# A decoder trunk's SSD layer: old states read four at a time, the first gate's tiles between the third group's, and the convolution's history by DMA

## The chip, the cores and the metric

The kernel runs on one core of one Trainium2 chip and is launched once. The metric is the device time of that core in microseconds (us); lower is better. Three runs of the kernel before took 1497.01, 1497.63 and 1501.10 us (median 1497.63). The profiled execution took 1500.51 us.

## The reference

The program is one inference step of a decoder trunk with four layers: a mixer with mLSTM and GLA heads, an MLP, a Mamba-2 (SSD) mixer, and an MLP, each followed by a layernorm of the scaled residual. It works on a prompt of 512 tokens and, at the same time, on 8 sequences ("samples") that each bring 4 new tokens and their old states. All 544 tokens pass through the same weights. The change is in the SSD mixer and in the last layernorm. The mixer computes, with 32 heads of 64 in 4 groups of 8 heads, a state of 128, and a causal convolution over 4 tokens:

```python
z, xbc, dtr = _split(x @ w_in, (SSD_INNER, SSD_CONV_DIM, SSD_HEADS))     # 2048, 3072, 32
cat = jnp.concatenate([conv0, xbc], axis=1)                              # 3 old inputs ahead
conv = conv_b
for w in range(SSD_CONV):
    conv = conv + cat[:, w:w + T] * conv_w[w]
new_conv = cat[:, T:]                                                    # an output
xs, Bm, Cm = _split(jax.nn.silu(conv), (2048, 512, 512))
dt = softplus(dtr + dt_bias);  a = dt * -exp(a_log)
# per chunk, with cs = cumsum(a), h0 the state before it
w = exp(cs[t] - cs[s]) (s <= t) * dt[s]
y = (Cm @ Bm^T * w) @ x  +  (Cm @ h0) * exp(cs)
h = exp(cs[-1]) * h0 + sum(exp(cs[-1] - cs) * dt * x * Bm)               # an output
y = (y + d_skip * xs) * silu(z), normed by group, @ w_out
```

For a sample the chunk is its 4 tokens, and h0 is its own old state: per group of heads a matrix of 128 x 512 floats (256 KB), 8 of them for the 8 samples.

## The kernel before

Activations lie with features on the partitions and tokens along the free side: a tile is 128 features x 544 tokens (512 of the prompt and 32 of the samples), done in two halves of 272 tokens. A dense product of one 128 x 128 weight block with one half is three matmuls of split operands (`dense`, line 367: high x high, low x high, high x low parts). One weight tile of the SSD's input product is 8 such blocks and two halves: 48 matmuls. The weight tiles come by DMA on SP's queue into three raw buffers (`WeightStream`, line 165); ACT makes the high part (line 166) and DVE the low part (line 167).

The stages follow each other: the first mixer (to about 240 us), an MLP (to about 650), the SSD's input product and its chunks (653 to about 1000), its output product, a second MLP, and the last layernorm (from 1486).

In the SSD stage the order of the instructions on TensorE (PE) is the order in which the program writes them (`manual_schedule` for PE). On the other engines, and on the DMA queues, a planner that simulates a timeline sets the order. The program writes dense matmuls, and `tick()` ahead of each of them counts down in "lanes": generators of small work (`dt`, `ssd`, `smp`, `norm`) that yield the number of dense matmuls until they go on (the table `W`: 72 at the start of a group, 14 between chunk steps, 26 between sample steps, 48 ahead of the samples' outputs). A lane works on one generator at a time; the next one in the same lane waits behind it. `until(key)` goes through lanes at once until a result is there.

The weight tiles of the input product come in the order: dt, then for each group g four tiles of x, one of B, one of C. Behind the third group's come the four z tiles of `gate(0)`, then the fourth group's six, then the z tiles of gates 1, 2 and 3. `gate(g)` makes z, its SiLU and the product with Y of group g.

- `ev_conv` (lines 1502 to 1533) is the way out of PSUM for x, B and C: ACT copies the two halves into a tile `ci` that holds three zeros, the prompt, and per sample three old inputs and four new ones (lines 1511, 1514, 1516); POOL fills in the old inputs from `cv0` (1510), and stores the new history to `ncp` and `cv0` (1520, 1521); ACT makes the first tap (1524), DVE three more (1526), and both make the SiLU (1529 to 1532). There are two `ci` buffers. `cv0` is read by one DMA ahead of the stage; two DMAs at the end of the stage write both histories out.
- `group` (1538 to 1661) does one group's four chunks of 128 tokens, and as a fifth block (b = 4) the 32 tokens of the samples. `scores(b)` loads the decay sums broadcast from a DRAM scratch tensor (`E`, line 1563, and for b = 1 to 3 two DMAs for `ec`, line 1568, all on ACT's queue), transposes x (`xt`, 1571), multiplies C and B (`cb`, 1573), and makes the masked matrix E. `state(b)` carries the state (1607, 1610), `outputs(b)` makes y (`yp`, 1632; added to Y at 1635).
- `samples` (1663 to 1697) works through the 8 samples of a group, two per step. A step loads two old states `h0` (line 1670; four buffers) and the same in the other layout, `h0n` (1672), waits 26 dense matmuls, multiplies C with the two old states into rows 64 to 127 of one PSUM tile `it` (1679; 32 rows each, the products of all steps added up: the matrix `Cm` is zero outside the tokens of its sample), makes the state update (`sps`, 1686), adds it on DVE (1692) and writes the new states from POOL's queue (1693). Rows 64 to 127 of `it`, times exp(cs) (`ecs`), go into the lower half of the tile z of block 4 (1694); the lower half of its E holds two unit matrices (`seye`), so that the 16 instructions of `outputs(4)` add the old states' share in the same products.
- `last_layernorm` (474 to 554) makes sums with PE, then works on ACT, DVE and POOL in an order written by hand (`do`, line 525), and issues the output DMAs (552 to 554).

## Time and profile before

| | us |
|---|---|
| median of 3 runs | 1497.63 |
| profiled execution | 1500.51 |
| its span (first to last instruction) | 1498.8 |
| PE busy in the span | 1473.0 |
| DVE busy | 1097.6 |
| ACT busy | 793.8 |
| POOL busy | 226.6 |

All times below are microseconds from the start of the span. An engine's busy time counts its instructions, not its register work or its DMA issues; a "q" behind an engine's name (ACTq, SPq) is its sequencer, where DMA issues and waits are seen. PEld is the load of a weight block into PE, which overlaps the matmuls. "<-DVE h0n L1692" behind an idle time says that it ended when DVE's instruction of line 1692 on the tile h0n was done. The granted clock is the share of full speed that TensorE's clock had in a stretch. fp32 matmuls appear as two instructions each.

### The profile page before, as it was taken

Reading aid. Unit: us, or ns where it says so; the run is one execution under the profiler, and the core shown is the slowest. Engines: PE = TensorE matmul, PEld = TensorE weight load, DVE = VectorE, ACT = ScalarE, POOL = GpSimd, SP = SyncE. Lnnn points to the kernel's source line nnn. Section 1 sums busy time; section 2 is a strip of 40 time slices with the busy share of each in tenths; the row PEclk is TensorE's granted clock in tenths of the full one; section 3 lists DMA queues with packets and bytes.
Section 4 is the critical chain, followed back from the end, with each engine's and each line's share of the span. In section 5 each row is a group of like instructions: output and inputs, shape, how many; then the busy total and the mean of one; then the engine's idle time right before and its main releaser. Section 6 shows DMA issues by size and latency. Waiting matters only on the chain.

```text
span 1498.8 us, 29214 instructions
## 1 busy us (share of the span) xinstructions
PE 1473.0 (98%) x11637; PEld 1423.6 (95%) x11637; DVE 1097.6 (73%) x2072; ACT 793.8 (53%) x1747; POOL 226.6 (15%) x295
## 2 busy tenths in 40 slices
PE   9999999999999999999999999999999999999997
PEld 9999999999999999999888788899999999999996
DVE  4956576886776766578898988777688677676656
ACT  5645556573554453457875675555257354444333
POOL 0511231100000000014444353421010000000000
PEclk9999999999999999999999999999999999999998
DMA  6321325223332232434566766364222233233121
GB/s 226 94 71 58 117 71 168 69 71 97 98 99 86 98 99 58 154 131 130 134 182 195 239 178 217 99 213 143 72 75 71 95 100 99 86 99 99 58 85 60
DMA packets 88225, 172.11 MB, mean 115 GB/s; under 512 B 9224, under 2 KB 43656, under 8 KB 87832
## 3 DMA queue, kind: packets, MB, share of 16 engines
q1 hardware_dynamic: 54968, 139.81, 30.1%
q10 hardware_dynamic: 29760, 17.46, 4.5%
q0 software_dynamic: 3360, 12.98, 2.2%
q8 instruction: 91, 1.49, 0.4%
q14 instruction: 46, 0.38, 0.1%
HBM read 153.48 MB, written 16.73 MB: 114 GB/s over the span
## 4 chain that ended last, share of the span: by engine, by line
PE 89%; DVE 5%; DMA 3%; ACT 2%; issue 1%; POOL 0%; ACTq 0%; DVEq 0%; POOLq 0%
PE psd L367 61%; PE psd L562 18%; DMA E<-d_cs 2%; PE num L812 1%; PE yp L1632 1%; PE gs L1043 1%; DVE acc L1526 1%; PE sp L1610 1%; DVE wlo L167 1%; PE it L1679 1%; PE ip L1607 1%; ACT whi L166 1%; PE sps L1686 1%; PE supd L950 0%; DMA d_ecs<-rows 0%
## 5 line engine op out<-in xcount | busy, mean ns | idle before, releaser
L367 PE MATMUL psd<-xh,whi 128*128 128x272 f32 x1504 | 446.2, 297 | 2.4 <-ACT ci L1516 2.1
L367 PE MATMUL psd<-xh,wlo 128*128 128x272 f32 x1504 | 440.1, 293 | 0.6 <-DVE wlo L167 0.6
L367 PE MATMUL psd<-xl,whi 128*128 128x272 f32 x1504 | 438.3, 291 | 1.5 <-DVE xl L451 1.3
L367 PE MATMUL psd<-hh,whi 128*128 128x272 f32 x1024 | 295.9, 289 | 0.7 <-ACT hh L286 0.7
L367 PE MATMUL psd<-hlo,whi 128*128 128x272 f32 x1024 | 295.5, 289 | 0.2
L367 PE MATMUL psd<-hh,wlo 128*128 128x272 f32 x1024 | 295.4, 288 | 0.0
L367 PEld LDWEIGHTS psd<-xh,whi 128*128 128x128 f32 x1504 | 283.8, 189 | 9.8 <-issue 5.1
L367 PEld LDWEIGHTS psd<-xl,whi 128*128 128x128 f32 x1504 | 284.3, 189 | 7.5 <-issue 4.2
L367 PEld LDWEIGHTS psd<-xh,wlo 128*128 128x128 f32 x1504 | 283.7, 189 | 4.8 <-issue 2.8
L167 DVE TENSOR_TENSOR wlo<-wraw,whi 128x1024 fp32r<-128x1024 f32 (+2 forms) x173 | 207.4, 1200 | 60.0 <-ACT whi L166 59.1
L166 ACT CAST whi<-wraw 128x1024 fp32r<-128x1024 f32 (+2 forms) x173 | 174.2, 1011 | 131.8 <-PE psd L367 114.4
L367 PEld LDWEIGHTS psd<-hh,whi 128*128 128x128 f32 x1024 | 192.8, 188 | 1.3 <-ACT hh L286 1.2
L367 PEld LDWEIGHTS psd<-hlo,whi 128*128 128x128 f32 x1024 | 192.8, 188 | 0.8 <-DVE hlo L287 0.6
L367 PEld LDWEIGHTS psd<-hh,wlo 128*128 128x128 f32 x1024 | 192.7, 188 | 0.1
L401 DVE TENSOR_TENSOR xf<-xf,psd 128x272 f32<-128x272 f32 x208 | 88.1, 432 | 76.0 <-PE psd L367 75.4
L562 PE MATMUL psd<-xh,wlo 128*128 128x272 f32 x416 | 119.9, 288 | 0.0
L562 PE MATMUL psd<-xh,whi 128*128 128x272 f32 x416 | 119.8, 288 | 0.0
L562 PE MATMUL psd<-xl,whi 128*128 128x272 f32 x416 | 119.6, 288 | 0.0
L202 ACT CAST whi<-wsum 128x1024 fp32r<-128x1024 f32 x52 | 54.3, 1044 | 111.3 <-PE psd L562 70.1
L202 ACT CAST whi<-wraw 128x1024 fp32r<-128x1024 f32 (+1 forms) x52 | 43.4, 834 | 95.3 <-PE psd L367 84.2
L203 DVE TENSOR_TENSOR wlo<-wsum,whi 128x1024 fp32r<-128x1024 f32 x52 | 63.7, 1224 | 23.2 <-ACT whi L202 23.2
L562 PEld LDWEIGHTS psd<-xl,whi 128*128 128x128 f32 x416 | 78.4, 188 | 0.0
(477 smaller groups left out, 2820.8 us busy)
## 6 DMA issues: line engine op xcount, KB each, us to landing
wraw<-mlp_w SPq DMA_DIRECT2D x80, 512.0 KB, 3.7
wraw<-ssd_in SPq DMA_DIRECT2D x40, 512.0 KB, 4.0
wraw<-mlp_w SPq DMA_DIRECT2D x64, 256.0 KB, 3.0
wraw<-ab_in SPq DMA_DIRECT2D x24, 512.0 KB, 3.7
h<-h SPq DMA_DIRECT2D x32, 256.0 KB, 3.9
h0n<-h0n SPq DMA_DIRECT2D x16, 512.0 KB, 4.5
E<-d_cs ACTq DMA_DIRECT2D x16, 512.0 KB, 4.3
s_h<-h0n POOLq DMA_DIRECT2D x16, 512.0 KB, 4.3
```

The source lines that it names most:

```text
L166: nc.scalar.copy(hi[:, r], w[:, r])
L167: nc.vector.tensor_tensor(lo[:, r], w[:, r], hi[:, r].bitcast(F32), ALU.subtract)
L202: self.cut[0] = nc.scalar.copy(hi, x).ins
L203: self.cut[1] = nc.vector.tensor_tensor(lo, x, hi.bitcast(F32), ALU.subtract).ins
L367: last[0] = TE.matmul(ps[:, :TH], wt[:, k, :], rt, start=i == 0, stop=i == n - 1).ins
L401: V.tensor_tensor(x, x, ps, ALU.add)
L562: last[0] = TE.matmul(ps, wt[:, k], bt[:, k], start=first and n == 0, stop=n == 11, skip_group_check=not first).ins
L812: TE.matmul(num[i], sT[:, i] if j == i else sT[:, (4, 7, 9)[j] + i - j - 1], vt[key][:, j, h, :w], start=j == 0, stop=j == i)
L1043: TE.matmul(p[:, 2 * m * b:2 * m * (b + 1)].rearrange("p (e t) -> p e t", e=2), z[:, 2 * m * b:2 * m * b + P], zq[:, :, m * b:m * (b + 1)] ...
L1526: V.scalar_tensor_tensor(acc[:, :n], ci[:, w:w + n], cw[:, m, w:w + 1], acc[:, :n], ALU.mult, ALU.add)
L1607: TE.matmul(ip[:, j * P:(j + 1) * P], hT[:, j * P:(j + 1) * P], Cf[:, tk], start=True, stop=True)
L1610: TE.matmul(sp, Bt[:, b], xw, start=True, stop=True)
```

## The change

Five parts are changed together.

1. Old states are read four at a time: in every second sample step four matmuls go to four blocks of 32 rows of `it` (0 to 127), and none in the others. `it` times `ecs` (now for four blocks of rows) goes into a tile `zs` of its own, taken from the `h0` buffers, and `outputs(4)` has eight more matmuls, `zs` with `seye`, accumulated with the former ones. E and z of block 4 become tiles that are zeroed once; the copies of `seye` and the zero fills per group go.
2. `gate(0)` becomes a generator. The weight order of the third group was x, x, x, x, B, C, launch of the group's chunks, z, z, z, z; it is now x, x, x, x, z, B, z, C, z, z, launch. The host lays out the weights in that order.
3. The convolution's old inputs come per tile by a DMA on SP's queue straight into `ci` (128 rows of 56 floats; the host leaves zeros for the new ones), issued when the tile before leaves PSUM; a DMA per tile on SP's queue writes the last 59 columns of `ci` out. The three POOL copies, `cv0` and `ncp` go, as do the two end DMAs and the load of `cv0`. `ci` has three buffers instead of two.
4. The two `ec` DMAs of group 0's block 1 are issued on SP's queue instead of ACT's.
5. In the last layernorm the mean is subtracted from the tiles 2 to 7 ahead of and behind the variance instead of after the inverse root, and one tile's scaling goes from ACT to DVE.

```diff
@@ -532,7 +532,10 @@
         do(S, "activation", sh, mu[:, :n], AF.Identity, scale=-1.0 / D)
-        do(V, "scalar_tensor_tensor", v, var[:, :n], 1.0 / D, ms, ALU.mult, ALU.subtract)
+        for k in (2, 4, 6):
+            do(V, "scalar_tensor_tensor", x[:, k:k + 2], pair(mu, k), -1.0 / D, x[:, k:k + 2], ALU.mult, ALU.add)
+            if k == 2:
+                do(V, "scalar_tensor_tensor", v, var[:, :n], 1.0 / D, ms, ALU.mult, ALU.subtract)
@@ -540,10 +543,8 @@
         for k in (2, 4, 6):
-            do(V, "scalar_tensor_tensor", x[:, k:k + 2], pair(mu, k), -1.0 / D, x[:, k:k + 2], ALU.mult, ALU.add)
-        for k in (2, 4, 6):
...
-        for k, eng in ((2, S), (3, S), (4, S), (7, V), (6, V), (5, V), (0, S), (1, S)):
+        for k, eng in ((2, S), (3, S), (7, V), (6, V), (5, V), (4, V), (0, S), (1, S)):
@@ -1386,16 +1387,14 @@
         V.tensor_scalar(prm[:, :136], prm[:, :136], 0.5, None, ALU.mult)
-        cv0 = pool.tile([P, 24, NB, 3], F32, name="cv0", bufs=1)
-        nc.sync.dma_start(out=cv0, in_=a["conv0"])
...
-        return con, prm, cv0, Cm
+        return con, prm, Cm
...
-        con, prm, cv0, Cm = consts
+        con, prm, Cm = consts
@@ -1413,6 +1411,10 @@
         ecs = pool.tile([P, 32], F32, name="ecs", bufs=1)
+        E4 = pool.tile([P, 8, NS], F32, name="E4", bufs=1)
+        z4 = pool.tile([P, 512], F32, name="z4", bufs=1)
+        G.memset(E4, 0.0)
+        G.memset(z4, 0.0)
@@ -1495,19 +1497,30 @@
             V.tensor_copy(csp, p2[:NS, :32])
-            for r in (64, 96):
+            for r in range(0, P, NS):
...
+        corder = [m for g in range(4) for m in (*range(4 * g, 4 * g + 4), 16 + g, 20 + g)]
+        inputs = {}
+        def place(i):
+            if i < len(corder):
+                ci = inputs[corder[i]] = cpool.tile([P, NC], F32, tag="ci", name="ci", bufs=3)
+                G.memset(ci[:, 0:3], 0.0)
+                nc.sync.dma_start(out=ci[:, NX:], in_=a["conv0"][corder[i]])
+        place(0)
...
-                    ci = st["ci"] = cpool.tile([P, NC], F32, tag="ci", name="ci", bufs=2)
-                    G.memset(ci[:, 0:3], 0.0)
-                    G.tensor_copy(ci[:, NX:].rearrange("p (b t) -> p b t", t=7)[:, :, 0:3], cv0[:, m])
+                    ci = st["ci"] = inputs.pop(m)
+                    place(corder.index(m) + 1)
@@ -1516,9 +1529,7 @@
                 ci = st["ci"]
-                cis = ci[:, NX:].rearrange("p (b t) -> p b t", t=7)
-                G.tensor_copy(ncp[:, m], ci[:, NX - 3:NX])
-                G.tensor_copy(cv0[:, m], cis[:, :, 4:7])
+                nc.sync.dma_start(out=a["convs"][m], in_=ci[:, NX - 3:])
@@ -1558,14 +1569,14 @@
                 else:
-                    tls[b] = pool.tile([P, 8, NS], F32, tag="E4", name="E4", bufs=1)
-                    E = tls[b][:NS]
+                    tls[b] = E4
+                    E = E4[:NS]
...
-                        S.dma_start(out=ec[64 * e:64 * e + 64], in_=d_ecs[8 * g + e:8 * g + 8:2, tk][None].broadcast_to([64, 4, n]))
+                        (S if g or b > 1 else nc.sync).dma_start(out=ec[64 * e:64 * e + 64], in_=d_ecs[8 * g + e:8 * g + 8:2, tk][None].broadcast_to([64, 4, n]))
@@ -1574,8 +1585,7 @@
                 else:
-                    z = pool.tile([P, 512], F32, tag="z4", name="z4", bufs=1)
-                    G.memset(z[NS:2 * NS], 0.0)
+                    z = z4
@@ -1591,9 +1601,6 @@
                 V.tensor_tensor(E, E, cb[:n, None, :n].broadcast_to([n, 8, n]), ALU.mult)
-                if b == 4:
-                    G.memset(tls[b][NS:2 * NS], 0.0)
-                    G.tensor_copy(tls[b][64:], seye[64:, None, :].broadcast_to([64, 8, NS]))
@@ -1629,7 +1636,9 @@
                         r = 2 * j + e
-                        TE.matmul(ypv[64 * e:64 * e + 64, j], z[:, 64 * r:64 * r + 64], E[:, r], start=True, stop=True)
+                        TE.matmul(ypv[64 * e:64 * e + 64, j], z[:, 64 * r:64 * r + 64], E[:, r], start=True, stop=zs is None)
+                        if zs is not None:
+                            TE.matmul(ypv[64 * e:64 * e + 64, j], zs[:, 64 * r:64 * r + 64], seye, start=False, stop=True)
@@ -1658,26 +1667,27 @@
             S.copy(Cm.rearrange("p (q r) -> p q r", r=NS + LS)[:, :, :LS], Cf[:, NP:].rearrange("p (q l) -> p q l", l=LS))
-            launch(samples(g, X, outputs, tls[4][2], Bs, Xs), "smp")
-        def samples(g, X, outputs, z, Bs, Xs):
+            launch(samples(g, outputs, Bs, Xs), "smp")
+        def samples(g, outputs, Bs, Xs):
...
-                h0 = [pool.tile([P, 512], F32, tag="h0", name="h0", bufs=4) for _ in range(2)]
+                h0 = [] if q % 4 == 0 else h0
...
-                    nc.sync.dma_start(out=h0[k], in_=a["h0"][g, q + k])
+                    h0.append(pool.tile([P, 512], F32, tag="h0", name="h0", bufs=4))
+                    nc.sync.dma_start(out=h0[-1], in_=a["h0"][g, q + k])
...
-                for k in range(2):
-                    TE.matmul(it[64 + NS * k:64 + NS * k + NS], Cm[:, NS * (q + k):NS * (q + k) + NS], h0[k],
-                              start=q == 0, stop=q == NB - 2)
+                if q % 4 == 2:
+                    for k in range(4):
+                        TE.matmul(it[NS * k:NS * k + NS], Cm[:, NS * (q - 2 + k):NS * (q - 1 + k)], h0[k], start=q == 2, stop=q == 6)
@@ -1691,10 +1701,11 @@
                 nc.gpsimd.dma_start(out=a["s_h"][g, q // 2], in_=hn)
-            V.tensor_tensor(z[64:].rearrange("p (h c) -> p h c", h=8), it[64:].rearrange("p (h c) -> p h c", h=8),
-                            ecs[64:, heads, None].broadcast_to([64, 8, 64]), ALU.mult)
+            zs = pool.tile([P, 512], F32, tag="h0", name="zs", bufs=4)
+            V.tensor_tensor(zs.rearrange("p (h c) -> p h c", h=8), it.rearrange("p (h c) -> p h c", h=8),
+                            ecs[:, heads, None].broadcast_to([P, 8, 64]), ALU.mult)
...
-            outputs(4)
+            outputs(4, zs)
@@ -1759,6 +1770,10 @@
         def gate(g, beside=()):
+            for _ in gate_tiles(g, beside):
+                pass
+        def gate_tiles(g, beside=()):
@@ -1775,11 +1790,12 @@
                     beside[i]()
-            square(g, *order[-1])
+                if i == len(order) - 1:
+                    square(g, *order[-1])
+                if i % 2:
+                    yield
...
-            if g == 3:
-                gate(0)
@@ -1799,6 +1815,9 @@
                     post()
+                if g == 2:
+                    first = gate_tiles(0)
+                    next(first)
@@ -1807,13 +1826,13 @@
                 post()
+                if g == 2:
+                    next(first) if m < 20 else list(first)
...
-        nc.sync.dma_start(out=a["p_conv"], in_=ncp)
-        nc.sync.dma_start(out=a["s_conv"], in_=cv0)
@@ -1995,7 +2014,9 @@
     z = [list(range(4 * g, 4 * g + 4)) for g in range(4)]
-    o["ssd_in"] = b[tiles[0] + tiles[1] + tiles[2] + z[0] + tiles[3] + z[1] + z[2] + z[3]]
+    t = tiles[2]
+    mixed = t[:4] + [z[0][0], t[4], z[0][1], t[5], *z[0][2:]]
+    o["ssd_in"] = b[tiles[0] + tiles[1] + mixed + tiles[3] + z[1] + z[2] + z[3]]
@@ -2004,7 +2025,9 @@
     o["ssd_prm"] = prm
-    o["conv0"] = i["state_ssd_conv"][0].reshape(NB, 3, 24, P).transpose(3, 2, 0, 1)
+    c = np.zeros((24, P, NB, 7), w.dtype)
+    c[..., :3] = i["state_ssd_conv"][0].reshape(NB, 3, 24, P).transpose(2, 3, 0, 1)
+    o["conv0"] = c.reshape(24, P, 7 * NB)
```

## Rows read from the trace of the kernel before

**Rows 1.** The page of the profile, part 1 (busy time, share of the span, number of instructions of each engine) and the engines' line of part 4 (the chain of work that ended last, shares of the span).

```profile
PE 1473.0 (98%) x11637; PEld 1423.6 (95%) x11637; DVE 1097.6 (73%) x2072; ACT 793.8 (53%) x1747; POOL 226.6 (15%) x295
...
PE 89%; DVE 5%; DMA 3%; ACT 2%; issue 1%; POOL 0%; ACTq 0%; DVEq 0%; POOLq 0%
```

**Rows 2.** The chain of waits in order of time, one step of it in the first MLP's second product: start, length (us), engine, tile and line, number of instructions.

```profile
392.32 10.53 PE psd L562 x84
```

**Rows 3.** The table by stretches: stretch and its length in us, then the busy time and number of instructions of PE, of PE's weight loads, of DVE, ACT and POOL, the mean granted clock of PE, the mean busy share of the DMA engines, GB/s.

```profile
769.00:827.00 58.00, 55.52 (x434) 46.47 (x433) 51.51 (x92) 36.11 (x111) 25.38 (x37) 1.00 0.66 204
827.00:855.00 28.00, 24.30 (x156) 18.82 (x155) 26.42 (x53) 19.05 (x54) 13.37 (x17) 0.94 0.77 236
...
889.00:920.00 31.00, 31.00 (x238) 26.86 (x238) 25.98 (x56) 16.52 (x42) 12.01 (x25) 1.00 0.79 260
...
1486.00:1498.80 12.80, 2.41 (x12) 1.39 (x10) 5.98 (x12) 5.02 (x11) 2.67 (x2) 0.71 0.23 88
```

**Rows 4.** The timeline of PE between 762 and 930 us: start, us from the first start to the last end, engine, line, operation, out<-in, tile sizes, number of instructions [idle time before, and what ended it].

```profile
762.97 1.09 PE L1632 MATMUL yp<-E,z 128*64 128x128 f32 x16 [0.86 <-DVE ec L1608]
...
828.70 1.05 PE L1679 MATMUL it<-h,Cm 128*32 128x512 f32 x4
...
838.59 0.60 PE L1547 MATMUL Btp<-scon,Bf 128*128 128x128 f32 x4
...
841.66 0.63 PE L1571 MATMUL xt<-scon,Y 128*128 128x128 f32 x4 [2.37 <-DVE h0n L1692]
843.04 0.77 PE L1573 MATMUL cb<-Cf,Bf 128*128 128x128 f32 x2 [0.75 <-DVE h0n L1692]
...
845.55 1.32 PE L1679 MATMUL it<-h,Cm 128*32 128x512 f32 x4
...
929.27 0.49 PE L1573 MATMUL cb<-Cf,Bf 128*128 128x128 f32 x2 [0.98 <-DVE Cf L1531]
```

**Rows 5.** All instructions of line 1679 (count: minimum/median/maximum ns, first and last start, forms); then PE's timeline at one of the sample steps, and at the old states of the mLSTM in the ab stage (line 916), with the columns of rows 4.

```profile
L1679 PE MATMUL it<-h,Cm x64: 592/605/889, 769.4 to 988.9; 128*32 128x512 f32 x64
...
890.53 1.05 PE L1679 MATMUL it<-h,Cm 128*32 128x512 f32 x4
891.51 0.74 PE L1686 MATMUL sps<-Bm,Xs 96*128 96x256 f32 x4
...
159.11 1.08 PE L916 MATMUL snum<-c,Zq 128*32 128x128 f32 x32
```

**Rows 6.** The timeline of PE at the sample's outputs of one group.

```profile
913.43 0.66 PE L1632 MATMUL yp<-E,z 128*64 128x32 f32 x16
914.01 0.39 PE L367 MATMUL psd<-xl,whi 128*128 128x272 f32 x1
```

**Rows 7.** The timeline of ACT (ACTq is its sequencer, here issuing DMAs) and, last, of PE around 720 us.

```profile
719.92 0.66 ACTq L1568 DMA_DIRECT2D ec<-d_ecs  x1
720.70 0.36 ACT L1514 COPY ci<-psd 128x240 f32<-128x240 f32 x1 [3.61 <-DMA d_ecs<-rows]
...
722.12 0.63 ACTq L1568 DMA_DIRECT2D ec<-d_ecs  x1
...
721.20 0.39 PE L367 MATMUL psd<-xh,whi 128*128 128x272 f32 x1 [2.07 <-ACT ci L1516]
```

**Rows 8.** Groups of instructions by line in 653 to 1021 us: line, engine, operation, out<-in with sizes, count | busy us, mean ns of one | idle of the engine just before them, and what ended it.

```profile
L1526 DVE SCALAR_TENSOR_TENSOR acc<-ci,sprm,acc 128x568 f32<-128x568 f32 x72 | 61.3, 858 | 0.7 <-ACT acc L1524 0.3
L167 DVE TENSOR_TENSOR wlo<-wraw,whi 128x1024 fp32r<-128x1024 f32 x45 | 56.5, 1257 | 12.1 <-ACT whi L166 12.0
...
L1692 DVE SCALAR_TENSOR_TENSOR h0n<-h0n,decs,sps 128x128 f32<-128x128 f32 x128 | 35.2, 339 | 3.4 <-PE sps L1686 2.2 <-DMA h0n<-h0n 1.1
...
L1520 POOL COPY ncp<-ci 128x3 f32<-128x3 f32 x24 | 17.6, 732 | 24.7 <-ACT ci L1514 20.0 <-ACT ci L1516 4.6
```

**Rows 9.** Waits of SP's queue over the span (who waited for whom: us in all, times, longest), one wait of ACT in 680 to 1010 us with the same columns, one kind of DMA issue (out<-in, queue, operation, count, KB each, median us to landing), and SP's timeline at the reads of old states.

```profile
SPq L165 <- DVE wlo L167: 539.9, 78, 28.6
...
SPq L1670 <- PE it L1679: 36.4, 11, 7.0
...
ACT ci L1514 <- DVE acc L1526: 1.7, 2, 1.2
...
E<-d_cs ACTq DMA_DIRECT2D x4, 32.0 KB, 4.4
...
891.61 6.24 SPq L1670 DMA_DIRECT2D h<-h  x4
```

**Rows 10.** The DMAs into the tile `h0` (which the profile names h), time from issue to landing.

```profile
DMA to landing us min/median/max: 2.6/3.9/8.1
```

**Rows 11.** The timeline of ACT and DVE in the last layernorm, columns as in rows 4.

```profile
1488.59 0.44 DVE L525 SCALAR_TENSOR_TENSOR lnq<-var,lnq 128x272 f32<-128x272 f32 x1 [1.36 <-PE var L530]
...
1488.95 1.98 DVE L525 SCALAR_TENSOR_TENSOR xf<-mu,xf 128x544 f32<-128x544 f32 x3
...
1489.62 0.40 ACT L525 ACTIVATE rp<-lnq 128x272 f32<-128x272 f32 x1
...
1490.85 1.97 DVE L525 TENSOR_TENSOR xf<-xf,rp 128x544 f32<-128x544 f32 x3
1491.59 2.63 ACT L525 ACTIVATE xf<-xf,lnp 128x272 f32<-128x272 f32 x5 [1.21 <-DVE xf L525]
...
1492.85 1.08 DVE L525 TENSOR_SCALAR xf<-xf,lnp 128x272 f32<-128x272 f32 x3
```

More of the change, by code (lines that the diff above doesn't have):

```diff
@@ L1407, in ssd @@
         dtb, al = prm[:32, 152:153], prm[:32, 153:154]
-        ncp = pool.tile([P, 24, 3], F32, name="ncp", bufs=1)
         NX = 3 + NP
@@ L1620, in state, with outputs @@
                     nc.sync.dma_start(out=a["p_h"][g], in_=hn)
-            def outputs(b):
+            def outputs(b, zs=None):
                 E, ec, z, xw = tls.pop(b)
@@ L2014 @@
             s_C=(P, 2, NB, P), s_n=(P, 2, NB), s_m=(4, NB), s_S=(P, 2, NB, P),
-            p_h=(4, P, 512), s_h=(4, NB // 2, P, 2, 512), p_conv=(P, 24, 3), s_conv=(P, 24, NB, 3))
+            p_h=(4, P, 512), s_h=(4, NB // 2, P, 2, 512), convs=(24, P, 3 + 7 * NB))
 def unlayout(r):
@@ L2028, in unlayout @@
                 s_h=r["s_h"].reshape(4, NB // 2, P, 2, 4, P).transpose(1, 3, 0, 4, 2, 5).reshape(1, NB, 32, 64, P),
-                p_conv=r["p_conv"].transpose(2, 1, 0).reshape(1, 1, 3, 3072),
-                s_conv=r["s_conv"].transpose(2, 3, 1, 0).reshape(1, NB, 3, 3072))
+                p_conv=r["convs"][:, :, :3].transpose(2, 0, 1).reshape(1, 1, 3, 3072),
+                s_conv=r["convs"][:, :, 3:].reshape(24, P, NB, 7)[..., 4:].transpose(2, 3, 0, 1).reshape(1, NB, 3, 3072))
 _ORDER = ("y_prompt", "y_sample", "p_C", "p_n", "p_m", "p_S", "p_h", "p_conv",
```

## The prediction

> **What bounds the kernel now.** I read the page's first part and its chain of waits [rows 1]: TensorE (PE) is busy 98% of the span and carries 89% of the chain, nearly all in dense products. In an undisturbed stretch of an MLP, 84 dense instructions take 10.53 us [rows 2], 0.1254 us each; one weight tile of the SSD stage, 48 of them, therefore takes 6.02 us. So an edit pays only if it takes work off PE, or closes one of PE's gaps: the span less PE's busy time is 25.8 us. The table by stretches [rows 3] says where: 10.4 us in the tail (12.80 less 2.41), 2.5 in 769-827, and 3.7 in 827-855, where the granted clock also averages 0.94. While old states are read (889-920) PE has no gap, and the DMAs move 260 GB/s.
>
> PE's timeline [rows 4] shows the gap of 827-855. Two instruction streams meet there: the sample steps of group 1 (`it` at 828.70 and 845.55) and the beginning of group 2 (Btp at 838.59, xt at 841.66, cb at 843.04). The longest of the idle entries, 2.37 and 0.75 us, wait for DVE's h0n updates, which stand in front of group 2's copies on DVE. Behind them PE runs slower for a while: the `it` step takes 1.32 us instead of 1.05. The mean clock of 0.94 over 24.3 us of work (rows 3) makes that some 1.6 us beside the 3.7 of idle: 5.3 in all.
>
> **Part by part.** The sum is made against the profiled execution, 1500.51 us (span 1498.8 and 1.7 around it), which is 0.19% over the median, 1497.63.
>
> 1. *States four at a time.* Now each of 16 steps has an `it` product of four instructions, two per state [rows 5]. One instruction lasts 605 ns (median), yet four end within 1.05 us and hold PE 0.98 us (890.53 to 891.51): two quadrants run side by side, in two passes. The ab stage shows four quadrants: 32 instructions in 1.08 us, one per 0.034 us; a single stream of that shape could not do this, as 16 instructions of 128 rows in two halves take 1.09 us in yp (762.97, rows 4). So I let a step of four states (eight instructions) take as long as two do now. Eight of 16 steps go, at 0.98 (1.07 with the join to dense work): **-8.0 us**, from -8.6 to -7.8; nothing hides it, because PE is the bound there.
>
> 2. *The price.* `outputs` for the samples gets 16 instructions per group (eight products, two each). Sixteen like them stand in the trace: 0.58 us from 913.43 to the next dense start at 914.01, 0.66 with their end [rows 6]. The new ones come one by one between them, half of whose slots may be lost: from 16 x 0.027 = 0.43 to double the row, 0.9. I take 0.47 per group, **+1.9 us**, +1.7 to +3.7. The product with `ecs` moves from 64 rows to 128 at the same length; the POOL fills and copy of group tiles go from a POOL that is 15% busy: nothing.
>
> 3. *Order of tiles.* Group 2 is launched after the four z tiles that stood behind its launch; as it also waited behind group 1 in its lane, its beginning comes some 150 dense instructions later by my count of slots (150 x 0.1254, about 19 us), against group 1's sample steps, which keep their place: the meeting of rows 4 goes, -5.3. But group 2 then has six dense tiles before group 3 is launched instead of ten, and its sample steps fall at group 3's beginning, where today cb waits 0.98 us for DVE's Cf (929.27). On DVE a conv tile has three passes of 0.858 and a weight split of 1.257, 3.8 us with smaller work behind them, below a tile's 6.02 on PE; a sample step adds 8 x 0.339 = 2.7 [rows 8]. A z tile has none of the three passes, so alternating evens DVE's load, but two streams are squeezed closer. Nothing in the trace decides how much returns: all of it and a second meeting of 2 us (+2 net), or nothing, and a fourth of the 2.5 us idle of 769-827 goes too (-6). I take half returned: **-2.5 us**.
>
> 4. *ec on SP.* ACT waits 3.61 us on the write of d_ecs before it can go on to evict (720.70), because the ec loads stand in its queue; PE is idle 2.07 us for that eviction at 721.20 [rows 7]. Moved to SP, which normally waits for a free weight buffer (539.9 us in 78 waits of the span, rows 9), the wait delays only loads that are ahead. Yet the four ec issues at 719.92 to 722.12 are those of two blocks, and the second block's stay on ACT: if the planner puts them as early, the wait stays. **-1.0**, -2.1 to 0. By the Trainium skill ("DMA: Bandwidth & Descriptors", section "Issuing engines are not separate DMA queues") a DMA begun on another engine saves only the sequencer's time to begin it. For two issues that would be 2 x 0.66 us off ACT, and with half of it reaching PE the sum would be 0.3 us less good; the trace shows the wait itself on the issuing engine, nearly three times the issues, and I go by the trace.
>
> 5. *Convolution's history.* 72 POOL copies go (the largest 24 take 17.6 us of POOL, rows 8), and 48 small DMAs come on SP. POOL is no bound; ACT's second evictions into ci wait 1.7 us in the stage for its buffers, held by DVE's passes [rows 9]. A load is placed one tile ahead, 6 us before the first eviction and 9 before the second, which needs it. The nearest small-row transfers, E's 32 KB, land in 4.4 us (rows 9). New on SP: a load waits for a buffer three tiles back, a store for the tile's last eviction; queued behind them are weight, h0 and h0n loads, which lead by tiles. The two end DMAs were beside work. **0**, from -1 (over half of ACT's 1.7 reaches PE and goes) to +2.1 (one load as late as the one of part 4, with its price on PE). The same page, section "Specifications", puts line rate at 512 B and more, below which a transfer reads, modifies and writes; these rows have 224 and 236 B. If that doubled E's 4.4 us, it would still be inside the 9, and the sum would stay; if it trebled them, it would be the +2.1.
>
> 6. *h0 in fours.* Four buffers hold one product; those of the second cannot be filled before the first has read them. SP's h0 issue already waits for `it` (36.4 us in 11 waits; four loads from 891.61 on are spread over 6.24 us, rows 9), and a load lands in 3.9 us median, 8.1 at most [rows 10]. Between the two products lie two steps of 26 dense instructions and one sps each, 2 x (26 x 0.1254 + 0.74) = 8.0 us, and what other lanes insert. **0** to +6.
>
> 7. *Tail.* In the last layernorm DVE is idle 1.36 us before its variance [rows 11]; one of the three mean subtractions (1.98/3 = 0.66) fits in there, the two others (1.32) run while ACT does Ln and Exp (until 1490.0), so that the products with rp begin at about 1490.3 instead of 1490.85; of the scalings ACT gets four instead of five (0.53 each) and DVE four instead of three (0.36 each), so that DVE ends last, at about 1490.3+1.97+1.44 = 1493.7 where ACT now ends at 1494.22. **-0.5**, -0.7 to 0.
>
> Sum: -8.0+1.9-2.5-1.0+0-0.5 = -10.1; 1500.5 becomes 1490.4. Brought to the median of the runs, 1497.63-10.1 = **1487.5 us**.
>
> **Rivals.**
> - *The collision returns in full* at the beginning of group 3. For it: z tiles of the next gate lie there, as they lay at 838; against it: with z and conv tiles alternating before, DVE starts there with less behind it. Left are -8.0+1.9-0.5 = -6.6, with up to +2.1 of part 5: 1491 to 1493.
> - *The second four states come late* (the slower side). After the first product, 1 MB of h0 must land within 8 to 9 us, beside 1 MB of h0n, 1 MB of s_h written and one weight tile or two, E and ec: 3.5 to 4 MB, while the busiest stretch moved 260 GB/s, 2.3 MB in 9 us. PE would stand at the second `it` of each group, as it is queued in order. With 4 us it is +16-10.1 = +5.9, **1503.5 us**; it decides from 10.1/4 = 2.5 us per group. Against: not all of these fall into the same 9 us, and 889-920 shows PE without idle at that rate.
> - *Four quadrants do not run together*: part 1 is 0, and 1497.6+1.9-2.5-1.0-0.5 = 1495.5. The ab rows speak against it, but they are shorter.
> - *The gaps close elsewhere too*: with POOL's copies gone ACT keeps up with PE in 769-827 (2.5 us, rows 3), and nothing returns at group 3: 5 us more, 1482.
>
> **Chances.** Forecast 0.54, collision 0.19, late states 0.08, quadrants 0.09, more gaps closed 0.10. Range 1480 to 1495.5: it leaves out the late states, and half of the quadrants' case and little at the lower end. A difference below 0.3% (4.5 us) cannot be told from no change: faster means under 1493.1, which holds the forecast, more gaps, and two thirds of the collision, whose ends may lie higher: 0.77; the same 0.15; slower 0.08.
>
> **What would show it.** Right: the line of `it` still has 64 instructions, but in eight places, with eight in about 1.05 us; steps without it go from dense straight to sps; yp at the samples has 32 instructions in some 1.1 us. The idle entries of 829 to 844 are gone, and the clock of that stretch is 1.00; ACT shows no 3.6 us for d_ecs; the last output issue is half a microsecond earlier after the last product. Wrong: idle on PE before `it` released by a DMA into h (late states); eight `it` instructions in 2 us (quadrants); idle at Btp, xt or cb of group 3 released by h0n updates (collision); ACT waiting for a DMA into ci, or SP for the store of convs with a late weight load behind it (part 5).

## The result, and the profile after

The changed kernel took 1503.90 us (median of 7 runs) against 1497.01 of before (7 runs): ratio 1.0043, 95% interval [1.0030, 1.0057]. By the ratio that is 6.4 us slower, where 10.1 us less were forecast. A second measurement gave 1.0041 [1.0025, 1.0058] (run "again" below). The profiled execution took 1502.54 us (span 1500.8).

First the stages, read from the start times of the same instructions in both traces (dt's first work in the SSD input product, the table load on ACT behind the SSD stage, and the last sum of line 431, some 33 us before the end):

| us in the profiled execution | before | after | again | without part 1 |
|---|---|---|---|---|
| first mixer | 245.6 | 245.1 | 247.0 | 245.8 |
| first MLP, to dt | 421.0 | 421.0 | 421.0 | 421.0 |
| SSD stage | 352.3 | 355.6 | 356.3 | 346.7 |
| output product, second MLP | 446.1 | 446.0 | 446.0 | 446.1 |
| from that sum to the end | 33.7 | 33.0 | 33.0 | 33.0 |

The first mixer, which no part of the diff touches, varies by itself by some 4 us over the profiles of this case (244.3 to 248.5), so the SSD stage is what to read: +3.3 us, and 9 below that without part 1. The table by stretches of after, columns as in rows 3, and one line of before for the last stretch:

```profile
718.00:769.00 51.00, 48.12 (x385) 44.22 (x384) 48.59 (x69) 40.78 (x126) 17.91 (x21) 0.97 0.59 140
769.00:827.00 58.00, 53.43 (x439) 46.82 (x438) 52.22 (x92) 36.96 (x112) 18.95 (x21) 0.97 0.72 215
827.00:855.00 28.00, 26.25 (x203) 22.17 (x202) 25.51 (x55) 14.96 (x38) 9.55 (x11) 1.00 0.75 245
855.00:889.00 34.00, 34.00 (x291) 31.87 (x288) 27.13 (x38) 22.49 (x64) 7.63 (x9) 1.00 0.52 150
889.00:920.00 31.00, 31.00 (x258) 28.60 (x257) 28.25 (x49) 22.03 (x62) 9.79 (x8) 1.00 0.53 138
920.00:972.00 52.00, 46.81 (x378) 40.43 (x376) 38.51 (x70) 27.97 (x85) 18.20 (x19) 0.93 0.59 194
```

```profile
920.00:972.00 52.00, 51.02 (x413) 46.90 (x411) 40.38 (x61) 32.38 (x95) 22.26 (x19) 1.00 0.38 114
```

827-855 is as forecast: its clock is back at 1.00, and the meeting of rows 4 is gone. But 769-827 has 4.6 us of PE idle instead of 2.5, and 920-972 has 5.2 instead of 1.0, with a mean granted clock of 0.93 instead of 1.00. PE's timeline shows what stands there:

```profile
724.54 1.09 PE L1582 MATMUL xt<-scon,Y 128*128 128x128 f32 x4 [2.22 <-DVE ncs L1498]
...
770.46 0.71 PE L1696 MATMUL sps<-Bm,Xs 96*128 96x256 f32 x4 [1.33 <-DVE Xs L1667]
774.49 1.06 PE L1690 MATMUL it<-h,Cm 128*32 128x512 f32 x8
...
780.37 0.63 PE L1582 MATMUL xt<-scon,Y 128*128 128x128 f32 x4 [1.23 <-DVE h0n L1702]
...
813.36 1.09 PE L1639 MATMUL yp<-E,z 128*64 128x128 f32 x16 [1.20 <-DVE ec L1615]
...
842.78 2.15 PE L1690 MATMUL it<-h,Cm 128*32 128x512 f32 x6
846.68 1.04 PE L1690 MATMUL it<-h,Cm 128*32 128x512 f32 x2 [1.75 <-DVE zt L1719]
...
924.29 0.65 PE L1582 MATMUL xt<-scon,Y 128*128 128x128 f32 x4 [3.68 <-ACT Bt L1559]
926.32 0.80 PE L1584 MATMUL cb<-Cf,Bf 128*128 128x128 f32 x2 [1.38 <-DVE Cf L1542]
930.45 1.94 PE L1690 MATMUL it<-h,Cm 128*32 128x512 f32 x8
```

774.49 is part 1 as forecast: eight instructions in 1.06 us, against four in 1.05 (rows 5). At 842.78 the eight start in pairs, each pair when its old state has landed, and the last pair starts at 846.68: the fourth old state is late (the releaser printed, DVE's zt, had long been done; PE's weight loads in front of the last three pairs waited 0.31, 0.52 and 2.66 us for DMAs into h). At 930.45 it is something else: no load waits there, but each of the eight instructions lasts 1.06 us instead of 0.60, in a stretch from 925.6 to 932.4 with a granted clock of 0.50. The waits at 770, 780, 813 and 924 are new or larger, and lead back to DVE. For the largest, 3.68 us for ACT's Bt, follow the timelines of POOL and ACT:

```profile
920.49 0.53 POOL L1703 DMA_DIRECT2D s_h<-h0n  x1 [2.90 <-DVE h0n L1702]
921.04 3.20 POOL L1721 TENSOR_TENSOR Y<-Y,zt 128x272 f32<-128x272 f32 x2
```

```profile
923.04 0.43 ACT L1735 ACTIVATE sq<-Y 128x272 f32<-128x272 f32 x1 [4.36 <-POOL Y L1721]
923.38 0.38 ACT L1716 ACTIVATE zt<-psd 128x272 f32<-128x272 f32 x1
923.66 0.58 ACT L1559 COPY Bt<-Btp 128x512 f32<-128x512 f32 x1
```

On each engine these stand one behind the other, in the order of its program: PE waits for Bt, which stands on ACT behind a square that waits for POOL's product, which stands on POOL behind the issue of a state's write that waits for DVE's update of h0n. DVE itself is not waiting for a load here: from 911.8 to 924.9 its timeline has one idle entry, 0.25 us. Next, SP's queue around the late state, and the waits for loads in 653-1025 us (who waited for whom: us in all, times, longest):

```profile
834.18 0.34 SPq L1512 DMA_DIRECT2D ci<-conv  x1
837.34 0.33 SPq L165 DMA_DIRECT2D wraw<-ssd_in  x1
837.76 1.86 SPq L1680 DMA_DIRECT2D h<-h  x3
839.85 0.33 SPq L1682 DMA_DIRECT2D h0n<-h0n  x1
840.27 0.38 SPq L1680 DMA_DIRECT2D h<-h  x1
```

```profile
DVE h0n L1702 <- DMA h0n<-h0n: 7.7, 5, 4.1
...
PEld it L1690 <- DMA h<-h: 4.2, 4, 2.7
```

The buffers came free with the first product, at 834.7. The loads are issued from 837.76 to 840.27, behind a weight load that waits for a buffer, and take 4.6 to 5.5 us. DVE waits 7.7 us for h0n; before it was 1.1 (rows 8). More than half of the 7.7, 4.06 us, is one wait in the last group (at 991.99 us), behind which PE stands 0.49 us.

### The profile page after: what moved, and what is told of

Read it like the earlier page. It is cut to its first block, busy times and chain, and to the rows that moved or that the text cites. A ratio compares the mean times of both kernels' runs of the same rounds, so it can differ in the third digit from the quotient of the medians.

```text
span 1500.8 us, 29372 instructions
## 1 busy us (share of the span) xinstructions
PE 1470.3 (98%) x11701; PEld 1426.3 (95%) x11701; DVE 1101.4 (73%) x2073; ACT 792.4 (53%) x1748; POOL 182.1 (12%) x213
## 4 chain that ended last, share of the span: by engine, by line
PE 38%; DVE 4%; ACT 4%; DMA 3%; issue 2%; POOL 1%; ACTq 0%; SPq 0%; DVEq 0%; POOLq 0%
PE psd L367 26%; PE psd L563 9%; DMA E<-d_cs 1%; ACT E L1602 1%; DVE acc L1537 1%; PE yp L1639 1%; DVE h0n L1702 1%; DMA h0n<-h0n 1%; ACT whi L166 1%; DMA s_h<-h0n 1%; DVE wlo L167 1%; PE sp L1617 0%; DMA ec<-d_ecs 0%; ACT Y L1643 0%; DVE xf L525 0%
```

## The experiments

All ratios are to the kernel before, measured with each group of runs on its chip, with 95% intervals; 0.1% is 1.5 us.

**One part at a time.** Four kernels put together from the diff's parts: part 1 alone on the kernel before, and the changed kernel without part 1, 2 or 3.

> The kernel before with part 1 alone (old states four at a time, with its price in the outputs); all else as before. Own work by the rows: 8 x 0.98 us less, 2.1 us more, so -6 us if nothing comes late. Theory A (four buffers make the second four states late by themselves): the late loads give back about 5 us as in the changed kernel's profile (3.9 us at one product of group 1, 0.8 and 0.8 at two others), ratio about 0.999. Theory B (the states are late because the convolution's DMAs stand in front of them in SP's queue): no late product here, ratio about 0.996.

> The changed kernel without part 1: two old states per product again, all other parts kept. If part 1 is worth what the profile of the changed kernel adds up to (-8.2+2.1+5.5 of late loads), the time is about that of the changed kernel, ratio 1.0045 to the kernel before. If its products were worth their full 6 us on the chip it is about 1.008.

> The changed kernel without part 2: the first gate's four z tiles behind the third group's B and C again. Theory C (the new order moves the meeting of two groups' streams to 920 us and makes it dearer, about 8 us of idle and slow clock there, against 6.3 for the two meetings of before): 2 to 4 us less than the changed kernel, ratio 1.002 to 1.003. Rival (the order gains as forecast, 2.5 us, and the loss is elsewhere): ratio 1.006.

> The changed kernel without part 3: the convolution's history by POOL copies again, no small DMAs on SP. Theory B: the loads of h0 are issued earlier, the late second product at about 843 us goes and the start of groups has fewer late evictions: 4 to 6 us less, ratio about 1.000 to 1.001. Theory A: the late product stays, ratio 1.004.

Measured: part 1 alone 1.0006 [0.9992, 1.0021]; without part 1 0.9985 [0.9975, 0.9995]; without part 2 1.0038 [1.0023, 1.0053]; without part 3 1.0028 [1.0017, 1.0039]. Part 1 is the loss: 0.58% or 8.7 us within the change, and nothing gained alone, where its own work should give 6 us. I had expected the kernel without part 1 at 1.0045, since late loads and saved products nearly cancel in the profile; the rest of its cost must lie in the other waits. Parts 2 and 3 cannot be told from zero in its company. Theory B fell: part 1 alone, without the small DMAs, waits for h and h0n too (2.7 and 4.3 us, less than the 4.2 and 7.7 with them), and comes out at 1.0006 instead of 0.996.

**Loads and cover.** One set of four states for a group; h0n ahead of h0 in the program; 16 more matmuls before a group's first step; and the changed kernel again.

```diff
-                h0 = [] if q % 4 == 0 else h0
-                for k in range(2):
+                h0 = [] if q == 0 else h0
+                for k in range(2 if q < 4 else 0):
...
-                yield W["sq"]
+                yield W["sq"] + 16 * (q == 0)
```

> The changed kernel itself once more, for a second profile. The SSD stage (from its first dt work to the table load behind it) took 352.3 us in the profile of before, 355.6 in the changed kernel's and 346.7 without part 1. Every theory: ratio 1.004, SSD stage 355 to 358 us; if the waits for old states and for h0n sit elsewhere in this execution but add up alike, they come from DMA timing and not from one place in the order.

> The changed kernel with one set of four old states per group: the product of the second half reads the same four tiles, whose loads are left out (16 of 32 loads of 256 KB; the samples' y is not the reference's). PE's instructions are the same. Theory D (what part 1 costs is that 1 MB must be read between two products into the buffers that the first one held, in front of h0n in SP's queue): the waits for h and h0n go, the whole 6 us of the products are gained: ratio 0.994 to 0.996, SSD stage 341 to 344. Theory E (the cost is elsewhere: sps that waits for Xs since the covering product went, outputs in 32 instructions, the meetings of groups): ratio 1.001 to 1.004, stage 350 or more.

> The changed kernel with the load of h0n written ahead of the loads of h0 in each sample step. Theory F (h0n is late, 7.7 us of DVE waits against 1.1, because it stands in SP's queue behind h0 loads that wait for the product): DVE's waits for h0n fall to 1 to 3 us and 2 to 4 us of the time come back, ratio 1.001 to 1.002. Rival (the planner orders SP's queue whatever the program's order, or the DMA engines' traffic makes it late): within 1 us of the changed kernel, ratio 1.004.

> The changed kernel with 16 more dense matmuls (2 us) ahead of a group's first sample step, which has lost its covering product in front of sps. Theory G (the wait of sps for Xs, 1.3 us in the changed kernel's profile, 3.5 with part 1 alone, makes a good part of the loss): that wait goes, 1 to 3 us come back, ratio 1.002 to 1.003. Rival (it is a small symptom, the loads decide): ratio 1.004.

Measured: again 1.0041; one set 1.0010 [0.9995, 1.0024]; h0n first 1.0041 [1.0024, 1.0057]; more cover 1.0038 [1.0021, 1.0054]. The late second set is worth some 5 us, neither all nor nothing: the ratio lies at the lower edge of theory E, well above theory D. With one set PE never waits for h, but DVE waits 9.1 us for h0n, more than with it, and xt and cb at 921 and 926 us wait 3.63 and 4.02. The two changes of order did nothing. With more cover the first sps waits for Xs no longer, but 3.96 us of another wait stand at 868 us.

**The two h0n buffers.** 30 instead of 26 matmuls per step (`sq=30`); h0n loaded for two of four steps only, with and without one set of h0; the same without part 1.

```diff
-                hn = pool.tile([P, 2, 512], F32, tag="h0n", name="h0n", bufs=2)
-                nc.sync.dma_start(out=hn, in_=a["h0n"][g, q // 2])
+                hns = [] if q == 0 else hns
+                if q < 4:
+                    hns.append(pool.tile([P, 2, 512], F32, tag="h0n", name="h0n", bufs=2))
+                    nc.sync.dma_start(out=hns[-1], in_=a["h0n"][g, q // 2])
+                hn = hns[q // 2 % 2]
```

> The changed kernel with 30 dense matmuls instead of 26 ahead of each sample step, so that two steps take as long as two steps of before. Theory H (the pace of the sample steps is set by the two h0n buffers: read, update on DVE, write, read again, about 12 us for two steps; part 1 shortens two steps from 9.8 to 8.7 us and packs loads of h0 in between, so DVE waits for h0n with the next group's work behind it): the steps keep the old pace, waits for h and h0n fall, 3 to 6 us come back, ratio 0.9995 to 1.002. Rival (the pace is no matter; loads are late because of the four buffers): ratio 1.003 to 1.004.

> The changed kernel with h0n loaded only for the first two steps of a group; the other two update the same two tiles again (8 of 16 loads of 512 KB left out; the samples' new states are not the reference's). DVE's and PE's instructions are the same. Theory H: DVE never waits for h0n, the meeting at 920-930 us and the late starts shrink, 3 to 6 us come back: ratio 1.000 to 1.002; what stays is the late h0 (about 4.6 us by the run with one set). Rival: ratio 1.004.

> Both left out: one set of h0 per group and h0n loaded only for two steps of a group. If late h0 and late h0n together are the whole loss of part 1, its products are worth their 6 us: 6 us below the same without part 1 (run nq_ring_off). If something else holds (DVE's own work in these stretches, the product that no longer covers sps), it is within 2 us of nq_ring_off or above.

> The changed kernel without part 1 and with h0n loaded only for two steps of a group: the reference for the run both_off. Theory H: two states per product waits little for h0n as it is (2.7 us of DVE waits), so 0 to 2 us less than the kernel without part 1: ratio 0.997 to 0.9985.

Measured: sq30 1.0077 [1.0058, 1.0096]; half of the h0n loads 1.0006 [0.9995, 1.0016]; both 0.9996 [0.9986, 1.0007]; the reference without part 1 0.9996 [0.9988, 1.0005]. Theory H fell with the first: slower steps cost 5 us. Late h0n is worth 5.5 us, late h0 4.9, both together only 7: the same stretches wait for one or the other. The reference gained nothing by losing half of its h0n loads (0.9996; 0.9985 with all of them). And with both out of the way part 1 is level with its reference, although PE has 6 us less to do. The pages of the two profiles show where these went: PE is busy 1465.8 us with part 1 and 1471.6 without, and idle 29.4 and 23.5 us of nearly the same span (1495.2 and 1495.1). What the products save comes back as idle time of PE. In the late loads' place something else holds.

**DVE.** Half of the state updates left out (`for k in range(1)` around line 1702) in both members of that pair; every third weight tile's low part on POOL, without part 1 (the edit below); and parts 2, 4 and 5 alone.

```diff
-                nc.vector.tensor_tensor(lo[:, r], w[:, r], hi[:, r].bitcast(F32), ALU.subtract)
+                (nc.gpsimd if phase == "ssd" and self.done % 3 == 0 else nc.vector).tensor_tensor(lo[:, r], w[:, r], hi[:, r].bitcast(F32), ALU.subtract)
```

> As both_off (one set of h0, h0n loaded for two steps of a group only), and of each step's eight state updates on DVE four are left out (64 of 128, 0.34 us each, 22 us of DVE). Theory I (DVE holds the stage where two streams meet, so that what PE saves turns into waits for DVE): with DVE relieved part 1 becomes worth what its products save, 4 to 6 us less than nq_off_half. Rival (PE's order and the chain of a group hold, not DVE's load): within 2 us of nq_off_half.

> The reference for both_off_half: without part 1, h0n loaded for two steps of a group only, half of the state updates left out. Theory I: fewer waits at the groups' beginnings, 3 to 6 us less than nq_ring_off (ratio 0.9996), so 0.996 to 0.9975. Rival: within 1 us of nq_ring_off.

> The changed kernel without part 1, with every third weight tile's low part in the SSD input product made by POOL instead of DVE (13 or 14 of 41 tiles, 1.26 us of DVE each, 17 us in all; POOL is 30 to 40% busy there). Theory I: 2 to 4 us less than without part 1 alone (ratio 0.9985), so 0.996 to 0.997. Rival (POOL makes those tiles late, or slows DVE down): 0.9985 or more.

> Parts 2, 4 and 5 alone (order of tiles, ec on SP, last layernorm): no four at a time, convolution's history by POOL copies. If the small DMAs of part 3 cost as with part 1 (about 2 us by the run no_conv), ratio 0.997; if they help once part 1 is gone, since POOL and ACT are relieved, 0.999 to 1.000.

Measured: with part 1 0.9948 [0.9935, 0.9962], its reference 0.9954 [0.9941, 0.9966]; low parts on POOL 1.0092 [1.0078, 1.0105]; parts 2, 4 and 5 alone 1.0009 [1.0000, 1.0018]. DVE's load does bear on the stage's time: 64 updates less, 15 and 13 us of its busy time by the pages (not the 22 of the expectation, as updates overlap), give 6 to 7 us in either kernel, although DVE is "only" 73% busy. In the kernel without part 1 it is 99% busy where groups 0 and 1 meet (columns as in rows 3):

```profile
769.00:820.00 51.00, 50.76 (x405) 42.68 (x404) 50.55 (x90) 35.15 (x107) 19.82 (x24) 1.00 0.72 229
```

But theory I fell in its second half: with DVE relieved part 1 is still worth nothing. PE's idle entries in the run with part 1 and half of the updates:

```profile
771.54 0.71 PE L1699 MATMUL sps<-Bm,Xs 96*128 96x256 f32 x4 [1.33 <-DVE Xs L1667]
780.97 0.63 PE L1582 MATMUL xt<-scon,Y 128*128 128x128 f32 x4 [0.76 <-DVE h0n L1705]
...
827.63 0.71 PE L1699 MATMUL sps<-Bm,Xs 96*128 96x256 f32 x4 [1.04 <-DVE Xs L1667]
...
904.28 0.71 PE L1699 MATMUL sps<-Bm,Xs 96*128 96x256 f32 x4 [0.96 <-DVE Xs L1667]
918.29 0.63 PE L1582 MATMUL xt<-scon,Y 128*128 128x128 f32 x4 [2.33 <-DVE h0n L1705]
```

These are 6.4 us; the reference has no wait at these places. PE is ahead by what it saved, and stops at the next place where it needs another engine's result. DVE is the last to deliver it, but by this pair its updates alone do not hold it. The chain of waits between 715 and 935 us, followed back through both profiles of the pair, points at something else. In the reference 52.4% of it are dense products, 9.9% loads of E and 1.7% ACT's exponentials of E; with part 1 these are 34.0, 12.5 and 7.1%. Part of it, from the last outputs ahead of the wait at 827 us (start, us, what):

```profile
791.29 1.02 PE yp L1639 x16
...
792.36 8.45 DMA E<-d_cs
...
804.34 6.04 DMA E<-d_cs
...
811.95 1.90 ACT E L1602 x7
...
826.80 0.69 DVE Xs L1667
...
827.63 0.71 PE sps L1699 x4
```

E has two buffers of 512 KB; a load into one starts when yp has read it, and mask, exponentials and copies follow on POOL, ACT and DVE. Part 1 takes nothing out of that chain. No run changed E's loads or its buffers, so that this chain takes the 6 us is read from the trace and not shown by an experiment.

POOL was no way out: a low part took it 2.49 us (DVE 1.30 in the same run), the wait of xt at the beginning of the stage grew from 2.23 to 6.09 us, and DVE slowed down beside it: a pass of the convolution at 715.38, while POOL subtracts, took 2.72 us where their mean is 0.92.

**The product one step earlier.** The four loads asked for ahead of the first and third step, and the product there:

```diff
-                for k in range(2):
+                for k in range(4 if q % 4 == 0 else 0):
...
-                if q % 4 == 2:
+                if q % 4 == 0:
...
```

> The changed kernel with the product of four in the first and third sample step of a group instead of the second and fourth, its four loads all asked for ahead of that step. The instructions are the same. Theory J (the product used to cover the wait of the first sps for DVE's Xs): no wait of sps for Xs, 1 to 3 us back, ratio 1.002 to 1.0035. Rival (the wait for DVE only moves on to the next place, or the first product comes late for its loads): ratio 1.004 or more.

> As both_off_half (one set of h0, h0n for two steps of a group, half of the state updates left out), with the product of four in the first and third step. Theory J: the 3.3 us of waits for Xs go, 2 to 4 us below both_off_half and nq_off_half: ratio 0.9925 to 0.9940. Rival (PE meets DVE at the next place instead): 0.9945 to 0.9955.

Measured: it_early 0.9983 [0.9971, 0.9995], 0.6% or 9 us below the changed kernel with the same instructions, and a little faster than the kernel before. That is level with the changed kernel without part 1 (0.9985): the move takes back what part 1 had cost, and part 1 still gains nothing. Its page tells the same: PE is busy 1467.1 us and idle 26.4, against 1471.2 and 21.4 without part 1. The relieved kernel (off_half_early) measured 0.9960 [0.9948, 0.9972], no gain on 0.9948. Theory J named the place and not the size, and in the relieved kernel it fell. Its mechanism held in part only: the wait of sps for Xs falls from 1.33 to 0.31 us, but that of xt behind it grows from 1.23 to 2.41, as the rival said. In it_early's profile the SSD stage takes 345.4 us:

```profile
771.62 0.71 PE L1696 MATMUL sps<-Bm,Xs 96*128 96x256 f32 x4 [0.31 <-DVE Xs L1667]
781.53 0.63 PE L1582 MATMUL xt<-scon,Y 128*128 128x128 f32 x4 [2.41 <-DVE h0n L1702]
...
917.13 1.05 PE L1690 MATMUL it<-h,Cm 128*32 128x512 f32 x2 [1.37 <-DMA h<-h]
918.71 1.04 PE L1690 MATMUL it<-h,Cm 128*32 128x512 f32 x2 [0.53 <-DMA h<-h]
923.21 0.66 PE L1582 MATMUL xt<-scon,Y 128*128 128x128 f32 x4 [0.73 <-ACT Bt L1559]
```

```profile
920.00:972.00 52.00, 50.53 (x428) 45.09 (x427) 39.59 (x75) 31.42 (x93) 20.63 (x22) 1.00 0.51 165
```

The states still come late (917-919), but that wait lies ahead of the beginning of the next group, and by this profile the chain of DVE, POOL and ACT runs on under it: xt waits 0.73 us instead of 3.68, cb not at all, and the stretch 920-972 has a granted clock of 1.00 where the changed kernel's had 0.93.

## Why the prediction was wrong, step by step

- *Part 1, the products (-8.0).* The size was right: five of the eight steps take 1.00 us from start to sps (the other three stand for late states or run at the slow clock). The step that failed is "nothing hides it, because PE is the bound there". PE's 98% is a mean. Where two groups' streams meet, PE stops for other engines at xt, cb, yp and sps, and a microsecond saved before such a place is waited there: PE had 5.8 us less work and 5.9 us more idle time in the pair without late loads. By itself the part measured 1.0006, not 0.996, and with its loads and half of DVE's updates out of the way still nothing.
- *Its price (+1.9).* Right: the 64 new instructions take 2.1 us from start to start. Left out of the sum was that the old `it` product covered sps's wait for DVE's Xs; in rows 5 it stands in front of sps, and with it back in front (it_early) most of that wait goes, to return at xt.
- *Part 6 (0, to +6), h0 in fours.* The rival of late states was right in mechanism, and mis-sized: the delay is 3.9 us at one product of group 1 and 0.8 at the second of the last group, not 4 in each group (the slow product at 930.45 is the clock, not a load); leaving the second set out gives 5 us back. That h0n would be late too was not in the prediction, and leaving half of its loads out gives as much. Why it is late is open: written ahead of h0, or without the second set in front, DVE waits 6.5 and 9.1 us for it all the same.
- *Part 3 (-2.5), the order.* The meeting of rows 4 went. It came back at 920-930 dearer than forecast: 3.68+1.38 us of idle instead of 0.98, with the slow clock behind it. Without the new order the kernel is the same within the interval. So the rival of the returning collision held beside the one of the late states; I had weighed them as alternatives. The reading that an update adds 0.339 us to DVE was too dear: eight of them end within 2.2 us, as they overlap (35.2 us for 128 in the same row).
- *Part 4 (-1.0), ec on SP.* The wait of 3.61 us on ACT is gone, as the row and not the rule of the Trainium skill ("DMA: Bandwidth & Descriptors", section "Issuing engines are not separate DMA queues") had it. It gained nothing: 2.07 us at 721.20 became 2.22 us at 724.54, where xt waits for DVE's ncs.
- *Part 5 (0, -1 to +2.1).* Within the change nothing that can be told. Without part 1 it is a gain outside the range: 0.9985 with it, 1.0009 without, 3.6 us. The loads of 224-byte rows land in 2.8 us (median) and the stores in 2.1, below the 4.8 of the 256 KB loads. The Trainium skill's rule on transfers under 512 B (same page, "Specifications") would slow them down; at these sizes no such delay shows, and neither PE nor DVE nor ACT waits for a load into ci.
- *Part 7 (-0.5).* Not shown. The end was 0.7 us shorter here, and 33.0 us in 15 of the 18 kernels with the new order; but three of them have 33.4 to 33.8, and the two with the old order have 33.2 and 33.7. The first subtraction did not fit into DVE's idle time: it began behind ACT's two instructions (DVE waited 1.53 us) and moved the variance back.

```profile
1491.29 0.72 DVE L525 SCALAR_TENSOR_TENSOR xf<-mu,xf 128x544 f32<-128x544 f32 x1 [1.53 <-ACT lnq L525]
...
1491.93 0.43 DVE L525 SCALAR_TENSOR_TENSOR lnq<-var,lnq 128x272 f32<-128x272 f32 x1
```

Added up: part 1 with its price was to give -6.1 us and cost 8.7 within the change, 14.8 of the 16.5 us between forecast and result; the other parts were to give -4.0 and gave -2.2 (0.9985). That the result lies next to the 1503.5 us of the rival of late states is luck: that sum has four waits of 4 us in it, and there was one.

What stays open: which chain takes up part 1's 6 us when neither loads nor half of DVE's updates are in the way. The profiles show the time as idle time of PE, and the chain of waits points at E's loads and exponentials, which no run changed. That PE's order, written by hand for the old lengths, brings it to other engines' results earlier fits every profile here, and it_early shows that the place of one product decides 9 us; a kernel with the order fitted anew to the shorter steps was not tried.

## What to carry to other kernels

A mean of 98% does not say that a saved instruction is a saved microsecond: look, stretch by stretch, for the next place where that engine takes another's result, and ask whether the other will be there earlier too. Work in front of a wait is cover; if it goes, the wait shows. Waits in one stretch stand in for one another (4.9 and 5.5 us gave 7), so test a part by leaving it out of the whole change and by adding it alone, and when an order is fixed by hand, move the changed piece by a step before giving it up: it was the difference between 1.0043 and 0.9983. Then compare with the change without that piece (0.9985 here): only this tells whether the piece gains anything.

## What was not expected of the hardware

A wait can cost more than its length. After 5 us of idle at 920-926 (with short work between), 15 dense matmuls ran for 3.4 us at a pitch of 0.23 us instead of 0.125, at the lower of the two clock levels, 1.2 GHz instead of 2.4, and so did the `it` product behind them; the stretch 920-972 had a granted clock of 0.93. By the same instructions without those waits (it_early) it was 1.00. And a subtraction of 128x1024 floats takes POOL 2.49 us, twice DVE's 1.26 (rows 8), and a pass of DVE beside it took 2.72 us instead of 0.92.
